# Moving background copies to another engine's DMA queue, and adding by transfer instead of by VectorE, in a one-core hybrid attention layer

## The chip, the core and the metric

The kernel runs on one core of a Trainium2 chip. The core has five engines with instruction streams of their own: TensorE (PE, matrix products; PEld are its weight loads), VectorE (DVE), ScalarE (ACT), GpSimd (POOL) and SyncE (SP). Each executes its stream in order and waits on semaphores. Sixteen DMA engines move data between the chip's memory (DRAM) and the core's SBUF; SP, ACT and POOL put transfers on queues for them. In the profile SP's transfers are on queue q1 (hardware_dynamic), POOL's on q0 (software_dynamic). An issued transfer runs by itself; whoever needs it waits until it has landed. The metric is the device time of one execution, in microseconds (us). Before the change its median is 899.32 us over three runs (899.3 to 900.65).

## The reference

One decoder layer in float32: 512 tokens, width 2048. Two groups of eight attention heads, one MLA and one FoX (with a forget gate), share one input projection `w_in` and one output projection `w_out`:

```python
h = _rms_norm(x, g_pre)
proj = h @ w_in
...
o_mla = _mla_branch(q_lat, kv_lat, k_rope_raw, g_q, w_uq, g_kv, w_ukv, cos, sin) * jax.nn.silu(gate_mla)
o_fox = _fox_branch(fq, fk, fv, f_logit, b_forget) * jax.nn.silu(gate_fox)
o = jnp.concatenate([o_mla, o_fox], axis=-1) @ w_out
return x + _rms_norm(o, g_post)
```

## The kernel before

**Three products for one.** Every float32 operand is split into a high part in PE's fast float format (`hi`, by a cast on ACT) and the rest (`lo`, by a subtraction on DVE). `mm3` (L149) then makes hi x hi, hi x lo and lo x hi, so a product step of 128 contracted rows for two output tiles is six matmuls. Weights go through this in chunks of 512 KB: `load` brings a chunk into a tile `raw`, `divide` casts it to `whi` (L277) and subtracts into `wlo` (L280). `whi` and `wlo` have three buffers each (pool `wp`), so the cast of a chunk writes where the cast three chunks earlier wrote. `chunk(i)` loads some four chunks ahead and divides two ahead of PE.

**Fewer block products.** The projections of the FoX values (v), the latents (l), the MLA gate (m) and the output (o, in two halves 0 and 1) are done as 2 x 2 block products by a scheme with seven products in place of eight. It needs sums of weight blocks:

- t7 = b12 + b22, t6 = b11 + t7, t4 = b21 + t6, t5 = b11 + b12 (up to signs, which the operand side carries).
- Most sums are made in the background in DRAM, each by a plain copy of the first block into a DRAM tile and a second transfer that adds the other block to it (`accum_op=ALU.add`). For v, l and m these are t7 and t6, 512 KB each, for four row pairs; for o they are t7, t6 and t4 over both halves, 1 MB each. They stand in the list `bg`, 36 steps.
- The sums t4 and t5 of v, l and m, and t5 of o, are made late: `load` brings the first block to `raw` and the second to a tile `second`, both on SP, and `join` adds them on DVE (L267). The products that use t5 of w_out are `("g5", 0)` and `("g5", 1)`, four chunks each.

**The pace of the background.** `paced` (L533) counts product steps; every `pace` of them (twice as many where the tile is 1 MB) it calls `add_step(n, mark)`. That call issues three things: the accumulate of step n - 1 on POOL (L310), the copy of step n on SP (L313), and a **mark** for step n + 1 on SP (L315). A mark is a transfer of 16 numbers from the `whi` tile that PE is using into the DRAM tile that the next copy will overwrite. Its data mean nothing: it makes the copy wait until the mark has landed, and the mark wait until that `whi` was cast, so that the background follows PE's progress. Since the mark reads `whi`, the cast that reuses its buffer must wait until the mark has landed. The pace is 20, 8 and 12 in the projections up to some 217 us, 4.9 in the FoX heads that follow (four product steps a chunk there), and 4.5 and 3 from some 560 us.

Within each engine and queue the order of instructions is set by a scheduler that goes by program order and readiness; `keep_in_program_order` (`in_order`, L132) fixes some of them. POOL's queue also has the transfers that put intermediate operands away in DRAM (`awaymg`, `awayoa`, `awayog`, `v_away`, `l_away`) and, at the end, adds of the residual x (L1600).

Of the kernel before, what the change touches and what calls it, by code (L numbers as in the profile page):

```python
# [16 lines left out]
ALU = mybir.AluOpType  # L17
# [49 lines left out]
def tile_hybrid_layer(  # L67
# [16 lines left out]
    nc = tc.nc  # L84
    pe, act, dve, pool = nc.tensor, nc.scalar, nc.vector, nc.gpsimd
# [14 lines left out]
    def slot(name, dt=F32, shape=(P, 2, S)):  # L100

        return sp.tile(list(shape), dt, tag="s", name=name)
# [13 lines left out]
    def split(src, name, scale=None, first=0):  # L116

        both = slot(name, F32R)
        hi, lo = both[:, 0, :], both[:, 1, :]
        split_into(hi[:, first:], lo[:, first:], src[:, first:], scale)  # L120
        return hi, lo
# [10 lines left out]
    def in_order(*instructions):  # L132

        for i in instructions:
            tc.keep_in_program_order(i)
# [72 lines left out]
    def add_chunks(w, cols, nk, per, width, first_k=0, single=0):  # L208


        first = len(chunks)
        k = 0
        while k < nk:
            n = min(1 if k < single else per, nk - k)
            chunks.append((w, cols, first_k + k, n, width))
            k += n
        return range(first, len(chunks))
# [6 lines left out]
    def raw_tile(i):  # L224
        if deep and deep[1] <= i < deep[2] and (i - deep[1]) % (DEEP + 3) < DEEP:
            return deep[0].tile([P, 1024], F32, tag="raw", name=f"raw{i}", bufs=DEEP)
        if i <= prods["g7", "v"][-1] and i % 5 < 2:
            return vr.tile([P, 1024], F32, tag="raw", name=f"raw{i}", bufs=2)
        pool = more[0] if more and (i - more[1]) % 6 < 3 else wp
        return pool.tile([P, 1024], F32, tag="raw", name=f"raw{i}", bufs=3)  # L230

    def load(i, small=None):

        w, cols, k, n, width = chunks[i]
        assert state["step"] >= needs.get(i, -3) + 2
        if cols is None:

            raw = raw_tile(i)
            to = raw if len(w.shape) == 2 else raw.rearrange("p (k c) -> p k c", k=2)
            nc.sync.dma_start(to, w)  # L240
            raws[i] = raw
            if k is not None:
                if seconds:
                    pool, bufs = seconds
                    second = pool.tile([P, 2, 512], F32, tag="second", name=f"second{i}", bufs=bufs)
                else:
                    second = slot(f"second{i}")
                nc.sync.dma_start(second, k)
                raws[i] = raw, second.rearrange("p k c -> p (k c)")
            return  # L250
        if i < 2:
            raw = slot(f"raw{i}", shape=(P, 1024))
        else:
            raw = raw_tile(i)
        v = raw[:, : n * width].rearrange("p (k c) -> p k c", k=n)
        for at, off, cnt in cols:
            (nc.sync if cnt >= P or small is None else small).dma_start(
                v[:, :, at : at + cnt],
                w[0, k * P : (k + n) * P, off : off + cnt].rearrange("(k p) c -> p k c", p=P),
            )  # L260
        raws[i] = raw
# [28 lines left out]
    def chunk(i, ahead_load=4, ahead=2):  # L290
        upto = i + ahead_load
        if deep:
            upto = max(upto, min(i + DEEP + 2, deep[2] - 1, state["loaded"] + i % 2))
        while state["loaded"] < min(len(chunks), upto + 1):
            load(state["loaded"])
            state["loaded"] += 1
        prepare(i + ahead)
        for k in range(i + ahead + 1, min(state["loaded"], i + ahead + (3 if deep else 2))):
            join(k)
        return ready.pop(i)  # L300

    W, made = {}, {}
    bg = []

    def add_step(n, mark):


        if n > 0:
            to, _, second = bg[n - 1]
            pool.dma_start(to.rearrange("p (k c) -> p k c", k=2), second, accum_op=ALU.add)  # L310
        if 0 <= n < len(bg):
            to, first, _ = bg[n]
            nc.sync.dma_start(to.rearrange("p (k c) -> p k c", k=2), first)  # L313
        if n + 1 < len(bg):
            nc.sync.dma_start(bg[n + 1][0][0:1, 0:16], mark)  # L315

    def sum_blocks(g, block, late, width=512):

# [14 lines left out]
    prods = {}  # L333
# [34 lines left out]
    first = add_chunks(w_in, [(0, O_KR - L4, KL), (KL, O_F, NH)], NK, 2, KL + NH, single=2)  # L368
# [81 lines left out]

    load_x_tile(0)
    load(0, act)
    load_x_tile(1)
    load(1, act)
    load_x_part(1)
    load(2, act)
# [76 lines left out]
    def paced(w):  # L533

        if state["step"] <= len(bg):
            state["tiles"] += 1
            wide = 0 <= state["step"] < len(bg) and bg[state["step"]][0].shape[1] > 1024
            pace = state["pace"] * (1 + wide)
            if state["tiles"] >= pace:
                state["tiles"] -= pace  # L540
                add_step(state["step"], w[0:1, 0, 0:16].bitcast(F32))
                state["step"] += 1
# [510 lines left out]
    def fox_k(p, wholes):  # L1053
        kb = [proj_bank(f"fk{p}{i}") for i in range(2)]
        proj_T(fox[p]["k"], [(kb[i], P, two[i]) for i in range(2)], hh, hl)
        k = []
        for i in range(2):
            t = tmp(f"fkt{p}{i}")
            dve.tensor_tensor(out=t, in0=kb[i], in1=rrow, op=ALU.mult)
            k.append(split(t, f"fk{p}{i}"))  # L1060
            whole_block(wholes, 2 + i, t)
        return k
# [164 lines left out]
    k = fox_k(0, wholes)  # L1227
# [27 lines left out]
    for p in range(4):  # L1255
        if p:
# [6 lines left out]
            k = fox_k(p, wholes)  # L1263
# [237 lines left out]
    for p in range(4):  # L1501
        c = mla[p]
# [46 lines left out]
        k = [[split(kb[i], f"mk{p}{i}"), tuple(keys_turned)] for i in range(2)]  # L1549
# [240 lines left out]
```

## Time and profile before

| | us |
|---|---|
| median of the timed runs | 899.32 |
| the profiled execution, whole | 901.18 |
| its span, first to last instruction | 899.4 |
| around the span | 1.8 |
| PE busy | 885.4 |
| DVE busy | 648.1 |
| ACT busy | 456.5 |
| POOL busy | 66.0 |

The page's second part cuts the span in 40 slices of 22.5 us; a digit is the busy share in tenths:

```profile
PE   9999999999999999999999999999999999999996
DVE  4579995548656636476588898965876885988786
ACT  6944434334344424335545565535565676646383
POOL 1010110011111201010000000000000000000021
DMA  9698798889899999896899884799743237789778
```

The rows of a wait view read: engine, line, what it waited for, us in total, times, longest. In a row of the timeline the first two numbers are the start and the duration, and the bracket holds the idle time before it and what ended it; an SPq row is an instruction of SP's queue. Where rows by stretches are shown, the columns are the stretch, its length, busy time and count (x) of PE, PEld, DVE, ACT and POOL, PE's granted clock, the DMA engines' mean busy share, and GB/s.

### The profile page before, as it was taken

To read this page: it belongs to the slowest core of one execution; us is meant where nothing else is said; L and a number is where in the kernel's file an instruction comes from. 1 tells how busy PE (TensorE), PEld (TensorE's weight loads), DVE (VectorE), ACT (ScalarE), POOL (GpSimd) and SP (SyncE) were. 2 spreads that over 40 slices of the span, in tenths; PEclk is the share of its full clock that TensorE was granted. 3 is DMA by queue.
4 is the path that set the end of the run, shared out by engine and by line. 5 is a ranking of instruction groups with operands and counts; after the bars stand their busy time and mean duration, and the time that the engine had idled before them with its cause. 6 is when DMAs were issued, how large, how long until landed. Compare 5 with 4: busy or idle time off the path is not lost.

```text
span 899.4 us, 12809 instructions
## 1 busy us (share of the span) xinstructions
PE 885.4 (98%) x4594; PEld 755.4 (84%) x4594; DVE 648.1 (72%) x1083; ACT 456.5 (51%) x830; POOL 66.0 (7%) x86
## 2 busy tenths in 40 slices
PE   9999999999999999999999999999999999999996
PEld 8988887888888888888998998788888888887885
DVE  4579995548656636476588898965876885988786
ACT  6944434334344424335545565535565676646383
POOL 1010110011111201010000000000000000000021
PEclk9999999999999999999999999999999999999999
DMA  9698798889899999896899884799743237789778
GB/s 299 223 268 238 207 336 283 248 225 315 256 278 274 250 246 256 249 251 174 278 411 395 318 299 134 154 232 219 208 101 125 63 118 227 228 320 319 264 214 252
DMA packets 126811, 219.31 MB, mean 244 GB/s; under 512 B 16506, under 2 KB 55188, under 8 KB 125724
## 3 DMA queue, kind: packets, MB, share of 16 engines
q1 hardware_dynamic: 114636, 180.52, 61.3%
q0 software_dynamic: 11376, 37.75, 20.0%
q8 instruction: 36, 0.59, 0.3%
q10 hardware_dynamic: 736, 0.22, 0.1%
q14 instruction: 27, 0.22, 0.1%
HBM read 203.77 MB, written 65.03 MB: 299 GB/s over the span
## 4 chain that ended last, share of the span: by engine, by line
PE 85%; DVE 5%; DMA 5%; ACT 3%; issue 1%; DVEq 0%; ACTq 0%; SPq 0%
PE fq L150 3%; PE fk L150 3%; PE fk L152 3%; PE fk L151 3%; PE fq L152 3%; PE fq L151 3%; PE in L586 3%; PE fg L150 3%; PE fg L151 3%; PE fg L152 3%; PE sm L629 2%; DMA second<-in_w_in_dram 2%; PE oa L152 2%; PE oa L151 2%; PE oa L150 2%; DVE wlo L280 2%
## 5 line engine op out<-in xcount | busy, mean ns | idle before, releaser
L280 DVE TENSOR_TENSOR wlo<-raw,whi 128x1024 fp32r<-128x1024 f32 (+3 forms) x217 | 257.1, 1188 | 139.2 <-ACT whi L277 128.1
L277 ACT CAST whi<-raw 128x1024 fp32r<-128x1024 f32 (+3 forms) x217 | 221.2, 1023 | 231.6 <-PE fk L151 35.4
L150 PE MATMUL fk<-h,whi 128*128 128x512 f32 x128 | 52.5, 410 | 0.0
L150 PE MATMUL fq<-h,whi 128*128 128x512 f32 x128 | 50.8, 397 | 0.0
L150 PE MATMUL fg<-h,whi 128*128 128x512 f32 x128 | 50.3, 393 | 0.0
L152 PE MATMUL fk<-h,wlo 128*128 128x512 f32 x128 | 50.2, 392 | 0.0
L151 PE MATMUL fk<-h,whi 128*128 128x512 f32 x128 | 50.1, 392 | 0.0
L152 PE MATMUL fq<-h,wlo 128*128 128x512 f32 x128 | 50.0, 390 | 0.0
L151 PE MATMUL fq<-h,whi 128*128 128x512 f32 x128 | 49.9, 390 | 0.0
L152 PE MATMUL fg<-h,wlo 128*128 128x512 f32 x128 | 49.9, 390 | 0.0
L151 PE MATMUL fg<-h,whi 128*128 128x512 f32 x128 | 49.8, 389 | 0.0
L647 ACT ACTIVATE pf<-pf,stf 128x128 f32<-128x128 f32 (+3 forms) x32 | 18.0, 562 | 61.1 <-DVE stf L638 61.1
L267 DVE TENSOR_TENSOR raw<-raw,second 128x1024 f32<-128x1024 f32 x32 | 39.0, 1218 | 2.6 <-DMA second<-in_w_in_dram 1.7
L586 PE MATMUL in<-whi,h 128*128 128x328 f32 x128 | 30.0, 321 | 0.0
L150 PE MATMUL mq<-ln,whi 128*128 128x512 f32 x72 | 28.7, 399 | 0.0
L152 PEld LDWEIGHTS fk<-h,wlo 128*128 128x128 f32 x128 | 24.0, 188 | 5.5
L152 PEld LDWEIGHTS fq<-h,wlo 128*128 128x128 f32 x128 | 24.0, 188 | 5.3
L151 PE MATMUL mq<-ln,whi 128*128 128x512 f32 x72 | 28.3, 393 | 0.0
L152 PEld LDWEIGHTS fg<-h,wlo 128*128 128x128 f32 x128 | 24.0, 188 | 5.1
L152 PE MATMUL mq<-ln,wlo 128*128 128x512 f32 x72 | 28.1, 390 | 0.0
L151 PEld LDWEIGHTS fg<-h,whi 128*128 128x128 f32 x128 | 24.1, 188 | 4.7
L150 PEld LDWEIGHTS fg<-h,whi 128*128 128x128 f32 x128 | 24.1, 188 | 4.7
(568 smaller groups left out, 2431.9 us busy)
## 6 DMA issues: line engine op xcount, KB each, us to landing
raw<-in_w_in_dram SPq DMA_DIRECT2D x96, 512.0 KB
raw<-in_w_out_dram SPq DMA_DIRECT2D x32, 512.0 KB
second<-in_w_in_dram SPq DMA_DIRECT2D x24, 512.0 KB
bmg<-awaymg SPq DMA_DIRECT2D x20, 256.0 KB
awaymg<-rmg POOLq DMA_DIRECT2D x8, 512.0 KB, 7.5
raw<-t6v SPq DMA_DIRECT2D x8, 512.0 KB
t7o<-in_w_out_dram SPq DMA_DIRECT2D x4, 1024.0 KB
t7o<-in_w_out_dram POOLq DMA_DIRECT2D x4, 1024.0 KB, 11.8
```

What stands on the lines that cost most here:

```text
L150: pe.matmul(o, ah, bh, start=first, stop=False, **kw)
L151: pe.matmul(o, ah, bl, start=False, stop=False, **kw)
L152: pe.matmul(o, al, bh, start=False, stop=last, **kw)
L267: tc.keep_in_program_order(dve.tensor_tensor(out=raw, in0=raw, in1=second, op=ALU.add))
L277: cast = act.copy(hi[:, :m], raw[:, :m])
L280: dve.tensor_tensor(out=lo[:, :m], in0=raw[:, :m], in1=hi[:, :m].bitcast(F32), op=ALU.subtract)
L586: pe.matmul(banks[t][:, :n], a[k][:, tss[t]], b[:, j, :], start=k == 0 and m == 0, stop=k == NK - 1 and m == 2,)
L629: pe.matmul(s[:, :nn], a[:, qs], c[:, :nn], start=(i == 0), stop=(i == len(pairs) - 1))
L647: act.activation(p, p, AF.Exp, bias=st[:, 0:1], scale=unit, accum_out=st[:, 1:2])
```

## The change

The mark and the background copies are issued by POOL, not SP. For chunks from `("g5", 0)` on, the second block of a late sum no longer goes to a tile `second`: it is a transfer on POOL that adds to `raw` in SBUF, and `join` finds nothing to do. No bytes to be read are added or taken away. All lines of the program after L242 stand two lines later, so L310, L313, L315, L277 and L280 become L312, L315, L317, L279 and L282.

```diff
             raws[i] = raw
-            if k is not None:
+            if k is not None and i >= prods["g5", 0][0]:
+                in_order(nc.gpsimd.dma_start(raw.rearrange("p (k c) -> p k c", k=2), k, accum_op=ALU.add))
+            elif k is not None:
                 if seconds:
...
         if 0 <= n < len(bg):
             to, first, _ = bg[n]
-            nc.sync.dma_start(to.rearrange("p (k c) -> p k c", k=2), first)
+            pool.dma_start(to.rearrange("p (k c) -> p k c", k=2), first)
         if n + 1 < len(bg):
-            nc.sync.dma_start(bg[n + 1][0][0:1, 0:16], mark)
+            pool.dma_start(bg[n + 1][0][0:1, 0:16], mark)
```

How that stands in the streams is seen at two places. The first is POOL in the FoX heads, from about 250 to 300 us. The names are t7m and t6m, the background sums of the MLA gate, with a number for the tile; awayoa are attention results put away. Before, POOL holds the accumulates and the away transfers alone:

```order
L310 DMA t7m_136<-in_w_in_dram 128x2x512
L310 DMA t6m_140<-t7m_136 128x1024
L310 DMA t7m_137<-in_w_in_dram 128x2x512
L310 DMA t6m_141<-t7m_137 128x1024
L310 DMA t7m_138<-in_w_in_dram 128x2x512
L925 DMA awayoa_4125<-gf_883 256x1x256
```

Now the marks (L317, from whi) and the copies (L315) stand between them:

```order
L312 DMA t7m_136<-in_w_in_dram 128x2x512
L317 DMA t6m_140<-whi_2454 16x1x1
L315 DMA t6m_140<-in_w_in_dram 128x2x512
L312 DMA t6m_140<-t7m_136 128x1024
L317 DMA t7m_137<-whi_2515 16x1x1
L315 DMA t7m_137<-in_w_in_dram 128x2x512
L312 DMA t7m_137<-in_w_in_dram 128x2x512
L317 DMA t6m_141<-whi_2564 16x1x1
L315 DMA t6m_141<-in_w_in_dram 128x2x512
L317 DMA t7m_138<-whi_2618 16x1x1
L312 DMA t6m_141<-t7m_137 128x1024
L315 DMA t7m_138<-in_w_in_dram 128x2x512
```

Mark, copy and accumulate of one sum now follow each other on one queue; at t6m_141 the next mark stands ahead of the accumulate.

From SP all marks and background copies are gone; the loads of `raw`, key rows, values and fetched operands are left there.

The second place is SP and POOL at the products with t5 of w_out. `raw` rows are first blocks, `second` rows second blocks, bog fetched operands, t7o sums read back. SP before:

```order
L240 DMA raw_7831<-in_w_out_dram 128x2x512
L248 DMA second_7784<-in_w_out_dram 128x2x512
L959 DMA bog_7804<-awayog_4345 128x512
L248 DMA second_7808<-in_w_out_dram 128x2x512
L959 DMA bog_7829<-awayog_4185 128x512
L248 DMA second_7833<-in_w_out_dram 128x2x512
L240 DMA raw_7853<-in_w_out_dram 128x2x512
L248 DMA second_7855<-in_w_out_dram 128x2x512
L240 DMA raw_7877<-t7o_152 128x2x512
```

SP now:

```order
L240 DMA raw_7828<-in_w_out_dram 128x2x512
L961 DMA bog_7803<-awayog_4345 128x512
L961 DMA bog_7826<-awayog_4185 128x512
L240 DMA raw_7848<-in_w_out_dram 128x2x512
L240 DMA raw_7870<-t7o_152 128x2x512
```

The second blocks are the last transfers on POOL ahead of the residual adds (L1602):

```order
L312 DMA t4o_163<-t6o_159 128x2048
L243 DMA raw_7782<-in_w_out_dram 128x2x512
L243 DMA raw_7805<-in_w_out_dram 128x2x512
L243 DMA raw_7828<-in_w_out_dram 128x2x512
L243 DMA raw_7848<-in_w_out_dram 128x2x512
```

Eight `second` loads have moved from SP to POOL, and eight additions are gone from DVE.

## The prediction

> **What bounds the kernel now.** I read the page's first lines, then busy time by stretches, then what TensorE (PE) waited for, then the queues SP and POOL on which the change works.
>
> ```profile
> PE 885.4 (98%) x4594; PEld 755.4 (84%) x4594; DVE 648.1 (72%) x1083; ACT 456.5 (51%) x830; POOL 66.0 (7%) x86
> 740.00:800.00 60.00, 60.00 (x277) 49.62 (x276) 46.83 (x59) 35.16 (x52) 0.00 (x0) 1.00 0.72 234
> 217.00:312.00 95.00, 94.68 (x445) 78.75 (x445) 60.11 (x134) 39.59 (x82) 16.67 (x18) 1.00 0.97 268
> 312.00:420.00 108.00, 108.00 (x526) 90.05 (x525) 63.32 (x144) 42.05 (x92) 8.84 (x10) 1.00 0.92 247
> 790.00:845.00 55.00, 54.27 (x238) 43.84 (x237) 46.01 (x52) 26.24 (x34) 0.00 (x0) 1.00 0.89 311
> ```
>
> PE is busy in 885.4 of 899.4 us at the full clock (1.00). 277 matmuls in 60 us are 0.217 us each, without idle time. So a copy or a sum that becomes cheaper elsewhere is worth only the PE waits that it ends:
>
> ```profile
> PE mix L1625 <- ACT scaler L1624: 2.2, 1, 2.2
> PE sm L629 <- DVE stm L638: 0.9, 1, 0.9
> PE vg L151 <- DVE wlo L280: 0.8, 1, 0.8
> PE od L151 <- DVE wlo L280: 0.7, 2, 0.4
> PE vg L150 <- ACT whi L277: 0.5, 1, 0.5
> PE vp L151 <- DVE wlo L280: 0.3, 1, 0.3
> ```
>
> Mix is the kernel's end. The others come to 3.2 us, which is all that can be won. Much can be lost, though: from 217 to 420 us the 16 DMA engines are 92 to 97% busy, and that is where the moved copies run.
>
> **Part 1, copies and marks on POOL: the new wait.** Before, a copy of step n+1 (SP) and the accumulate of step n (POOL) ran side by side. After, one queue in program order holds mark, copy, accumulate. A copy waits for its mark to land, an accumulate for its copy, and in the order shown above most marks stand behind the previous accumulate, whose 16 DMA engines they share. A step becomes a series: copy, then accumulate with the next mark. What each takes:
>
> ```profile
> 303.39 0.56 SPq L313 DMA_DIRECT2D t7m<-in_w_in_dram  x1
> 308.13 1.17 POOL L310 DMA_DIRECT2D t7m<-in_w_in_dram  x1 [2.67 <-DMA t7m<-in_w_in_dram]
> 293.31 0.56 SPq L313 DMA_DIRECT2D t6m<-in_w_in_dram  x1
> 304.55 0.91 POOL L310 DMA_DIRECT2D t6m<-t7m  x1 [8.38 <-DMA t6m<-in_w_in_dram]
> ...
> t6m<-t7m POOLq DMA_DIRECT2D x4, 512.0 KB, 7.1
> t7m<-in_w_in_dram POOLq DMA_DIRECT2D x4, 512.0 KB, 9.8
> awaymg<-rmg POOLq DMA_DIRECT2D x8, 512.0 KB, 7.5
> DMA to landing us min/median/max: 5.4/9.5/14.4
> ```
>
> The last row is for all of L310. A copy's landing lets the accumulate start: at most 4.7 us after issue (303.39 to 308.13), at most 11.2 in the other pair, which shared the engines with an accumulate. No trace row has a plain 512 KB copy on POOL from DRAM to DRAM; its nearest is awaymg, 7.5. I take 4.5, by the undisturbed pair, since no other background transfer runs beside it then. An accumulate takes 5.4 at the least, 7.1 (t6m) or 9.8 (t7m, issued 1.5 to 2.7 us behind another one). I take 6.5 for one that is alone. With 0.5 for two resumptions (an estimate) a serial step takes 4.5 + 6.5 + 0.5 = **11.5 us**, bounded by 9.9 (4.5 + 5.4) and 17.3 (7.5 + 9.8). Where the order puts the next mark and copy ahead of the accumulate's successor, a step costs about the accumulate, 7 us.
>
> The program asks for a step every 4.9 products' steps, four of which use up one cast weight chunk (whi):
>
> ```profile
> L277 ACT CAST whi<-raw x9: 1037/1048/1056, 255.2 to 311.0; 128x1024 fp32r<-128x1024 f32 x9
> L277 ACT CAST whi<-raw x6: 1037/1055/1056, 222.9 to 243.1; 128x1024 fp32r<-128x1024 f32 x6
> PE fk L151: 5.7, 4
> ```
>
> Nine casts from 255.2 to 311.0 are 6.97 us a chunk, so 6.97 x 4.9 / 4 = 8.5 us a step. That is shorter than 11.5: **POOL falls behind**. Between t7l_122's mark (cast at 222.9) and t7m_136's (243.1) four steps, mostly of the short kind, cost 4 x 7 = 28 us against 20.2: about 7 late. From there to t7o_152's mark are eight steps, six serial and two short: (6 x 11.5 + 2 x 7) / 8 = 10.4, so 8 x 1.9 = 15 more. That mark then lands 5 us after its issue, behind an accumulate. Sum: 27 us after its cast.
>
> Who waits for it: the mark reads whi, which has three buffers, so ACT's third cast after it cannot start before the mark has landed. That cast is due 3 x 6.97 - 1.05 = 19.9 us later. ACT is 27 - 20 = 7 us late, and behind the cast on ACT stand the exponentials (L647) and splits (L139) that PE's transposes and value products need. Today such a cast waits for PE alone (last row), and PE had none of these waits. I let PE see 6 of the 7 us.
>
> Two other things stand behind a waiting POOL. Its away transfers (awaymg, v_away, awayoa) come later by the same lag; before 217 us a step comes only every 20, 8 or 12 product steps of six matmuls (26, 10.4 and 15.6 us at 0.217 each), so there is hardly a lag for them to take over. And the sums themselves are read late:
>
> ```profile
> L240 SPq DMA_DIRECT2D raw<-t6m x8: 319/320/418, 456.9 to 531.1; - x8
> ```
>
> t6m's last accumulate, at 319 us today, may come 100 us later before its reader waits. Only the marks bite.
>
> The 1 MB steps that follow come at half the rate, every 17 us:
>
> ```profile
> t7o<-in_w_out_dram POOLq DMA_DIRECT2D x4, 1024.0 KB, 11.8
> t6o<-t7o POOLq DMA_DIRECT2D x4, 1024.0 KB, 10.5
> t4o<-t6o POOLq DMA_DIRECT2D x4, 1024.0 KB, 8.7
> ```
>
> Mean accumulate 10.3, a copy some 7 (4.5 plus half again, an estimate), 0.5 to resume: 17.8. The lag isn't worked off; 0.8 x 5 = 4 us more. The six later o steps, from 560 us, start with an idle POOL; I count them at nothing (bound: 0.8 us each, 5 us). **Loss: 6 + 4 = 10 us.** Ends: at 9.9 a step the lag stays under 20 and the loss is 0; at 13 (copy 5.8, accumulate 6.7) the eight steps add 24 in place of 15, the 1 MB ones some 10: 25 us; at 17.3 it would be over 50.
>
> The 72 added issues are nothing in themselves: POOL is 7% busy, and an issue takes 0.9 to 1.2 us (the POOL rows above).
>
> What SP wins: marks no longer block its loads, and copies don't precede them.
>
> ```profile
> SPq L313 <- DMA t7m<-whi: 21.2, 4, 10.0
> 119.96 11.23 DMA second<-in_w_in_dram
> 608.11 12.91 DMA raw<-in_w_ukv_dram
> ```
>
> The two loads, from the chain that ended last, landed late, and waits vg (1.3 us) and sm (0.9) follow them. At 607.5 a 1 MB copy went out on SP just ahead of the second. But the engines that carry these bytes stay the same, so I count half: -1.1 us. At worst nothing.
>
> The Trainium skill, "DMA: Bandwidth & Descriptors", section "Anatomy of one DMA — SWDGE (gpsimd) path", puts a POOL-issued DMA at about 2.0 us plus bytes / 436 GB/s. By this estimate 512 KB is 3.2 us, a serial step 6.4, and the loss 0, which is the first rival below. The trace has no accumulate under 5.4 us, so the measurement speaks against it.
>
> **Part 2, the last sums by adding transfers.** Eight DVE adds go, and eight loads `second` move from SP to POOL, where nothing else is queued (idle from 653 to 868 us).
>
> ```profile
> L267 DVE TENSOR_TENSOR raw<-raw,second x8: 1216/1218/1226, 796.8 to 841.0; 128x1024 f32<-128x1024 f32 x8
> 793.38 1.41 SPq L240 DMA_DIRECT2D raw<-in_w_out_dram  x1
> 807.62 1.22 DVE L267 TENSOR_TENSOR raw<-raw,second 128x1024 f32<-128x1024 f32 x1
> 809.00 1.05 ACT L277 CAST whi<-raw 128x1024 fp32r<-128x1024 f32 x1 [2.04 <-DVE raw L267]
> c<-in_x_dram POOLq DMA_DIRECT2D x8, 256.0 KB, 10.1
> ```
>
> The adds are 8 x 1.22 = 9.8 us of DVE, hidden today but for the od wait (0.7): DVE is busy 46 of 55 us. The price is that load and sum no longer run in parallel. The fourth chunk: load out at 794.8, landed after 4.7 (the copy's row), added 7 later (between 5.4 and 10.1, the accumulates above, nearer to t6m's 7.1): ready at 806.5, against 808.8 today. With 10.1 it is 809.6, 0.8 late. So I take **-0.7 us**, bounds -1.0 and +1.6 for both blocks. The other four chunks have some 10 us of room (loads from 816.5, adds from 829.8).
>
> **Sum.** 10 - 1.1 - 0.7 = +8 us on the span of 899.4, so 907.4; with the 1.8 us around the span (901.18 for the profiled execution) 909.2. The timed median, 899.32, is 1.9 under that execution, so I predict 899.3 + 8 = **907.3**.
>
> **Rivals.**
> - *POOL keeps up (faster).* If serial steps take under about 10 us, the mark lands inside the 19.9 us and PE waits for nothing new; the waits vg, sm, od and vp shrink: 899.3 - 2.5 = 896.8. For it: copies of 4.7, an accumulate of 5.4, and DMA engines relieved by the series itself. Against: 97% DMA. Chance 0.21.
> - *The two cancel.* Lag just over 20 us, loss 1 to 3, won 1 to 2, or the background was never on PE's path either way: 899. Chance 0.15.
> - *POOL is far behind.* Steps of 13 us or more, as the loaded rows (11.2 for a copy, 9.8 for an accumulate) have it: 899.3 + 25 - 1.8 = 923 and up. Chance 0.14, of which 0.08 above 926.
> - *DVE holds up POOL's issues.* If each issue had to wait for the DVE sum that runs then (1.22 us, the L267 row), two issues a step would add 2.4 us: the six serial steps 14 us more, 899.3 + 8 + 14 = 921 or so. Against it:
>
> ```profile
> L310 POOL DMA_DIRECT2D t7m<-in_w_in_dram x4: 1172/1172/1482, 263.8 to 308.1; - x4
> ```
>
> Four issues spread by 0.3 us while DVE was busy 63% of the time. Chance 0.03, taken out of the forecast's 0.50. The Trainium skill, "SBUF — State Buffer", section "SBUF: two separate sides", states such a rule: a DVE operation in a two-port mode locks GpSimd out of writing descriptors. By that rule alone the background would be the slower the more of it POOL issues; the row shows no trace of it.
>
> **How the numbers follow.** The forecast of a loss up to 25 us has 0.50 (0.03 of it by DVE), the far case 0.14: slower 0.64, same 0.15, faster 0.21. 0.2% (1.8 us) is about what a measurement of this kernel can tell from none. Range 896 to 926: it takes in the first rival's low end and steps up to 13 us, and leaves out the worst of the far case.
>
> **What would show it.** In the profile after: accumulates on POOL waiting for copies nearly back to back from 245 us; casts of whi waiting for DMA t7m<-whi, t6m<-whi or t7o<-whi between 290 and 410 us, and PE waits behind ACT there; if none, the lag argument falls. Accumulates into raw should land within 7 us, and od should have no wait. A copy on POOL that lands in 3.5 us, or an accumulate in 5, makes the prediction wrong on the fast side.

## The result, and the profile after

The changed kernel's median is **962.97 us** (960.86 to 963.98, four runs) against 899.99 us for the kernel before on the same chip (899.3 to 905.14, four runs): a ratio of 1.0684, 95% interval 1.064 to 1.0727. It is slower by some 63 us. The forecast was 907.3 with a range up to 926. The sign is right, and so is the mechanism of part 1; the size is far off, and part 2 lost time where a gain was forecast.

First what answers to the opening lines of the prediction: the page's busy time, and busy time by stretches in the FoX heads, which are later now.

```profile
PE 902.7 (94%) x4594; PEld 763.5 (80%) x4594; DVE 638.3 (67%) x1075; ACT 456.5 (48%) x830; POOL 119.8 (12%) x166
```

```profile
245.00:310.00 65.00, 54.94 (x248) 44.17 (x247) 28.07 (x67) 20.76 (x48) 12.97 (x18) 0.95 0.79 206
310.00:365.00 55.00, 43.09 (x192) 34.48 (x191) 19.81 (x43) 14.08 (x32) 11.82 (x17) 0.91 0.77 177
365.00:430.00 65.00, 54.11 (x240) 43.58 (x239) 29.06 (x68) 20.36 (x45) 8.77 (x12) 0.92 0.82 197
```

PE lacks 10, 12 and 11 us in these three stretches; before, it was full there. DVE and ACT are idler too (POOL isn't), and so are the DMA engines: 77 to 82% and 177 to 206 GB/s, where before they showed 92 to 97% and 247 to 268. So nothing is overloaded here; something waits. PE's largest waits:

```profile
PE pvf L150 <- ACT phf L139: 21.0, 5, 9.1
PE sf L631 <- ACT fw L127: 7.1, 1, 7.1
PE od L151 <- DVE wlo L282: 6.0, 8, 0.8
```

PE waits for splits (L139) and copies (L127) of ACT and for what comes of chunks that are ready late. ACT's own waits at the cast of `whi`:

```profile
ACT whi L279 <- issue: 61.9, 17, 10.9
ACT whi L279 <- DMA raw<-in_w_out_dram: 26.8, 8, 6.0
...
ACT whi L279 <- DMA t7m<-whi: 18.2, 2, 9.9
```

18.2 us are for marks by name, and 61.9 us are put down to "issue", a wait whose releaser the row doesn't name. The times at which the marks land name it: by the trace, 14 casts that stood between 249 and 411 us before start 0.06 to 0.16 us after a mark lands, and the five longest "issue" waits are theirs. The row of raw is part 2: all eight chunks with an adding transfer are waited for.

To see where the time arises I compare the two executions cast by cast: 217 casts of weights stand in the same order in both, and the delay is the start of a cast after less its start before. These are my differences, in us:

```
cast starts before at   211.2  270.2  311.0  364.8  420.7  459.1  613.2  634.8  785.6  814.0  838.8  882.4
delay after the change    2.1    5.9   26.5   45.0   50.7   52.6   53.1   50.8   50.5   55.0   58.6   59.6
```

Of the 52.6 us at 459, some 50 arise between 211 and 427 us, in the FoX heads; 2.3 come back from 621 on; 9.1 are added in the two t5 products of w_out at the end. The last delay is the difference of the spans, 959.1 - 899.4 = 59.7.

**How one lag turns into one delay.** Two marks show it, each with the cast before and after that is the third next behind it. First casts of the kernel before, on ACT: of the chunk whose whi t7o_152's mark reads (310.95) and its third next (330.26), then the same pair for the mark of t4o_161 (391.25, 410.73).

```profile
310.95 1.04 ACT L277 CAST whi<-raw 128x1024 fp32r<-128x1024 f32 x1
330.26 1.05 ACT L277 CAST whi<-raw 128x1024 fp32r<-128x1024 f32 x1 [0.84 <-PE fk L151]
391.25 1.05 ACT L277 CAST whi<-raw 128x1024 fp32r<-128x1024 f32 x1 [0.89 <-PE fk L151]
410.73 1.06 ACT L277 CAST whi<-raw 128x1024 fp32r<-128x1024 f32 x1
```

After the change, POOL's timeline with these two marks and the copies that follow them, and below it the two third next casts in ACT's timeline:

```profile
363.93 0.81 POOL L317 DMA_DIRECT2D t7o<-whi  x1
370.60 0.72 POOL L315 DMA_DIRECT2D t7o<-in_w_out_dram  x1 [5.86 <-issue]
...
453.07 0.97 POOL L317 DMA_DIRECT2D t4o<-whi  x1
...
463.09 0.71 POOL L315 DMA_DIRECT2D t4o<-in_w_out_dram  x1 [8.30 <-DMA t4o<-whi]
```

```profile
369.34 1.04 ACT L279 CAST whi<-raw 128x1024 fp32r<-128x1024 f32 x1 [9.38 <-issue]
...
462.87 1.05 ACT L279 CAST whi<-raw 128x1024 fp32r<-128x1024 f32 x1 [6.40 <-PE fg L152]
```

By the trace the marks land at 369.27 and 462.80; the casts start 0.07 us later. (The last row names PE, whose release came at 462.71; the wait in ACT's queue ahead of it ran from 455.92 until the mark landed.) The first mark lands 58.3 us after the time of its cast before, the deadline is 330.26 - 310.95 = 19.3, and the delay is 39.1. The second: 71.6 late, deadline 19.5, delay 52.1. The lag less the deadline is the loss. Where a cast starts as the mark lands, that sum comes out by itself; what the two casts show is that they do start there.

**Why the lag is so much larger than forecast.** POOL's timeline after, in two pieces: one as forecast, one not.

```profile
292.09 0.82 POOL L317 DMA_DIRECT2D t7m<-whi  x1
298.20 0.72 POOL L315 DMA_DIRECT2D t7m<-in_w_in_dram  x1 [5.29 <-issue]
302.69 1.17 POOL L312 DMA_DIRECT2D t7m<-in_w_in_dram  x1 [3.77 <-DMA t7m<-in_w_in_dram]
303.41 0.96 POOL L317 DMA_DIRECT2D t6m<-whi  x1
...
323.01 1.15 POOL L312 DMA_DIRECT2D t7m<-in_w_in_dram  x1 [7.37 <-DMA t7m<-in_w_in_dram]
323.73 1.88 POOL L927 DMA_DIRECT2D awayoa<-gf  x2
324.93 1.20 POOL L317 DMA_DIRECT2D t6m<-whi  x1
337.70 0.72 POOL L315 DMA_DIRECT2D t6m<-in_w_in_dram  x1 [11.57 <-DMA t6m<-whi]
...
342.65 0.84 POOL L317 DMA_DIRECT2D t7m<-whi  x1
```

From mark to mark, 292.09 to 303.41, is a serial step of 11.3 us: the accumulate with the mark behind it some 6.1, the copy 4.5. That is the step that the prediction worked out. But from 324.93 to 342.65 it takes 17.7: two away transfers stand between accumulate and mark, and the mark's 64 bytes landed 12.5 us after their issue. By the trace the four landed in the order of their issue, at 335.95, 336.60, 337.25 and 337.41; in the whole trace none of POOL's 151 transfers landed before one issued earlier. From t7m_136's mark (261.18) to t7o_152's (363.93) eight steps take 102.75 us, 12.8 each.

### The profile page after: what moved, and what is told of

Read it like the earlier page. It is cut to its first block, busy times and chain, and to the rows that moved or that the text cites. A ratio compares the mean times of both kernels' runs of the same rounds, so it can differ in the third digit from the quotient of the medians.

```text
span 959.1 us, 12763 instructions
## 1 busy us (share of the span) xinstructions
PE 902.7 (94%) x4594; PEld 763.5 (80%) x4594; DVE 638.3 (67%) x1075; ACT 456.5 (48%) x830; POOL 119.8 (12%) x166
## 4 chain that ended last, share of the span: by engine, by line
PE 45%; DMA 5%; issue 3%; DVE 2%; ACT 1%; POOL 0%; DVEq 0%; POOLq 0%; ACTq 0%
DMA raw<-in_w_out_dram 4%; PE sm L631 3%; PE oa L152 2%; PE oa L151 2%; PE oa L150 2%; PE mq L150 1%; PE mq L151 1%; PE mq L152 1%; DMA t4o<-whi 1%; PE od L151 1%; PE od L152 1%; PE ptm L658 1%; PE gl L150 1%; PE od L150 1%; PE mv L150 1%
## 5 line engine op out<-in xcount | busy, mean ns | idle before, releaser
L282 DVE TENSOR_TENSOR wlo<-raw,whi 128x1024 fp32r<-128x1024 f32 (+3 forms) x217 | 257.2, 1188 | 220.8 <-ACT whi L279 212.5
L279 ACT CAST whi<-raw 128x1024 fp32r<-128x1024 f32 (+3 forms) x217 | 221.1, 1023 | 311.0 <-issue 61.9
L150 PE MATMUL fq<-h,whi 128*128 128x512 f32 x128 | 52.3, 409 | 0.0
L151 PE MATMUL fq<-h,whi 128*128 128x512 f32 x128 | 51.0, 398 | 0.0
L269 DVE TENSOR_TENSOR raw<-raw,second 128x1024 f32<-128x1024 f32 x24 | 29.3, 1219 | 2.4 <-DMA second<-in_w_in_dram 2.4
L243 POOL DMA_DIRECT2D raw<-in_w_out_dram x8 | 9.5, 1188 | 164.8 <-DVE rog L885 123.8
L151 PEld LDWEIGHTS fq<-h,whi 128*128 128x128 f32 x128 | 24.9, 195 | 4.7
L150 PEld LDWEIGHTS fq<-h,whi 128*128 128x128 f32 x128 | 24.9, 194 | 4.7
L150 PEld LDWEIGHTS fk<-h,whi 128*128 128x128 f32 x128 | 24.7, 193 | 4.5
```

What stands on the lines that cost most here:

```text
L150: pe.matmul(o, ah, bh, start=first, stop=False, **kw)
L151: pe.matmul(o, ah, bl, start=False, stop=False, **kw)
L243: in_order(nc.gpsimd.dma_start(raw.rearrange("p (k c) -> p k c", k=2), k, accum_op=ALU.add))
L269: tc.keep_in_program_order(dve.tensor_tensor(out=raw, in0=raw, in1=second, op=ALU.add))
L279: cast = act.copy(hi[:, :m], raw[:, :m])
L282: dve.tensor_tensor(out=lo[:, :m], in0=raw[:, :m], in1=hi[:, :m].bitcast(F32), op=ALU.subtract)
```

## Experiments

Each stands against the kernel before (median 899.7 to 900.8, run beside it each time). p1 names copies and marks on POOL alone, with the last sums as before; p2 the last sums alone. In the kernels named p1 the lines keep their old numbers up to L315.

**The parts alone.** p1_only keeps the hunk in `add_step`, p2_only the one in `load`.

> Copies and marks on POOL, the last sums of w_out on VectorE as before. Theory A (POOL's series of mark, copy and accumulate lets the marks fall behind, and each late mark keeps a whi buffer from ScalarE's next cast): the delay of the changed kernel up to its 420th us of the old time, 52.6 us, less some 2 us won where a w_ukv load lands earlier: 899.5 + 50.5 = 950 us. Rival B (the adding transfers at the end cost most, or both parts only together): under 930 us.

> Only the last sums by adding transfers on POOL; copies and marks on SP as before. If the parts add up, casts of the eight chunks come 9 us later in all, as in the changed kernel: 908 us. If the 9 us there came from the background having been late, this is 899 to 900 us, or 898.5 as the prediction had it.

p1_only: 950.61 us (948.94 to 953.77), ratio 1.0548 (1.0516 to 1.058). p2_only: 909.13 (907.51 to 909.48), 1.008 (1.0057 to 1.0103). Both are as expected if the parts add up. Against 900.77 that is +49.8 and +8.4, together 58 of the 63 us. Part 1 delays the casts by 51.7 us at 459 and 49.5 after 635, part 2 adds nothing up to 785 us and 7.9 from there to the end. Both together showed 52.6 and 9.1 at these places.

**Copies or marks.** Each kernel moves one of the two to POOL:

```diff
copies_pool
-            nc.sync.dma_start(to.rearrange("p (k c) -> p k c", k=2), first)
+            pool.dma_start(to.rearrange("p (k c) -> p k c", k=2), first)
marks_pool
-            nc.sync.dma_start(bg[n + 1][0][0:1, 0:16], mark)
+            pool.dma_start(bg[n + 1][0][0:1, 0:16], mark)
```

> Of part 1 only the copies are on POOL; the marks are back on SP, so a late POOL no longer holds a mark and its whi buffer. Theory A: POOL still falls behind by tens of us, but TensorE does not wait for it: 897 to 901 us, no cast waits for a mark for longer than 2 us. Rival C (the copies on POOL's queue are slower, or crowd the DMA engines, and the weights come late): 930 to 950 us, as with both.

> Of part 1 only the marks are on POOL, behind the accumulates; the copies are back on SP. Theory A: marks again land behind accumulates and hold whi, but the copies run beside the accumulates, so a step takes some 8 to 9 us instead of 12: 5 to 30 us lost, 905 to 930 us. Rival C (it is the copies on POOL): 899 to 901 us.

copies_pool: 901.87 (897.68 to 904.19), ratio 1.0004 (0.9983 to 1.0024); its profiled execution is not late in the FoX heads (-1.5 us at 421), is 5.7 us later at 613 than at 459, and ends 2.3 late. marks_pool: 940.48 (937.64 to 942.11), 1.0428 (1.0399 to 1.0458), more than expected. So 36 copies of 0.5 or 1 MB on POOL's queue are in the median no loss and no gain that can be told; 36 transfers of 64 bytes there lose 40 us. With both there (p1_only) a mark also stands behind the copies, and the loss is 50.

**A fourth buffer for whi.** If the hold is what costs, one buffer more gives one chunk more.

```diff
-NSLOT = 28
+NSLOT = 27
-        hi = wp.tile([P, 1024], F32R, tag="whi", name=f"whi{i}")
+        hi = wp.tile([P, 1024], F32R, tag="whi", name=f"whi{i}", bufs=4)
```

> Copies and marks on POOL, last sums on VectorE, as in p1_only (950.6 us), with a fourth buffer for whi (and 27 slots in place of 28 elsewhere, to make room). Theory A (a mark holds its whi buffer until it lands, and the cast that wants the buffer is the third next): the deadline of every mark moves by one chunk, once, 6.97 us where it decides: 943.6 us, and the delay of the casts against before about 45.5 after 421 us in place of 52.4. Rival B (PE loses the time to the late background itself, by transfers that crowd or results that are missing, not by the hold): no change, 949 to 953.

943.66 us (941.76 to 945.75), the expected figure. The way there was less even: the delay is 5.4 us at 311 (p1_only 23.9), 36.9 at 421, 45.4 at 459 and 40.5 at the end, 10 under p1_only. The missing slot also shifts the work ahead of the FoX heads (-2.6 us at 211), and the last cast gains 10 us on p1_only's, the whole span only 7.3. So this run supports the hold, but that its time meets the expected figure to the digit is in part luck.

**A slower pace in the FoX heads.**

```diff
-    set_pace(4.9)
+    set_pace(7)
```

> As p1_only, but in the FoX heads a background step is asked for every 12.2 us (1.75 chunks) in place of 8.5. Theory A (the loss is the excess of the chain's time per step over the pace, less the deadline of 19.9 us): eight steps at 12.8 against 12.2 lose 5 us of lag, and the start lag of 15 us stays under the deadline with it; the chunks behind these lose little: 899 to 915 us, with casts delayed by under 15 us at 421 us. The price is that some steps move to later stages, where the pace isn't changed. Rival B (copies and marks on POOL cost PE time by themselves, whatever the pace): 940 to 950.

913.76 us (911.22 to 918.12), ratio 1.0156 (1.0126 to 1.0187): asked for less often, the same chain loses 17.8 us at 421 in place of 51.0. The time is inside the 899 to 915 expected, though the delay is over its 15 us: the eight steps from t7m_136's mark (273.41) to t7o_152's (383.71) take 13.8 us each here, not 12.8, and so miss the 12.2 asked by 13 us in all in place of the 5 reckoned.

**Marks that hold nothing, first try: a constant.**

```diff
-            pool.dma_start(bg[n + 1][0][0:1, 0:16], mark)
+            pool.dma_start(bg[n + 1][0][0:1, 0:16], ident[0:1, 0:16])
```

> As p1_only, but the mark reads a constant (the identity's first row) in place of the cast whi, so that it holds no buffer of the casts; the values that it writes are overwritten by the copy as before. What is left out is the pacing by TensorE's chunks: the chain runs as fast as POOL and the buffers of the sums let it. Theory A (the hold is the whole mechanism): the casts no longer wait for any mark, 895 to 910 us, the top end if the earlier start of the transfers crowds the loads. Rival B (the chain's own traffic or its lateness costs the time): 940 us and more.

1030.51 us (1027.34 to 1032.44): theory A's figure is missed, and the rival's "940 and more" takes it in, but by a cause that neither named. Without the pacing most of the series runs in the first third. ACT's waits up to 400 us:

```profile
ACT whi L277 <- DMA raw<-in_w_in_dram: 53.4, 10, 11.0
ACT smg L139 <- DMA awaymg<-rmg: 40.8, 1, 40.8
ACT L700 <- DMA awaymg<-rmg: 19.8, 1, 19.8
```

From 0 to 110 us the DMA engines are full (a share of 1.01, 0.85 before) and PE works 88 us, loads of weights come late, and two waits of 40.8 and 19.8 us are for away transfers that stand on POOL behind the series. All 133 us have arisen by the cast that starts at 364 us (231 before), none later. The run shows what the marks are for, but it leaves the question open, since no series was left where p1_only loses its time.

**Second try: the mark reads a copy.** The pacing stays, whi is free as soon as ACT has copied 16 numbers.

```diff
+            copied = cst.tile([1, 16], F32, tag="copied", name=f"copied{n}", bufs=8)
+            act.copy(copied, mark)
-            pool.dma_start(bg[n + 1][0][0:1, 0:16], mark)
+            pool.dma_start(bg[n + 1][0][0:1, 0:16], copied)
```

> As p1_only (950.6 us), but each mark reads a copy of 16 numbers that ScalarE takes of whi at the same place, in one of eight buffers of its own: the pacing by the chunks stays, the mark holds no whi. ScalarE gets 35 copies of some 0.1 to 0.2 us. Theory A (the hold of whi is the mechanism): the series on POOL still falls behind by about 10 us for each 3 steps, but no cast waits for a mark; 896 to 906 us, with the delay of the casts under 5 us at 421 us. Rival B (the late series itself costs TensorE, by crowding or by results that come late): 925 us and more, with waits for raw in place of those for marks.

939.3 us (934.16 to 944.7), ratio 1.0433 (1.0393 to 1.0473): by its time the rival is right and theory A wrong. The trace says something else. First the stretches, as shown for the changed kernel above:

```profile
245.00:310.00 65.00, 65.00 (x311) 54.18 (x310) 37.59 (x91) 26.84 (x65) 13.48 (x18) 1.00 0.86 218
310.00:365.00 55.00, 55.00 (x264) 45.64 (x263) 30.56 (x72) 21.96 (x52) 11.29 (x15) 1.00 0.78 199
365.00:430.00 65.00, 64.89 (x353) 55.59 (x352) 41.24 (x87) 28.74 (x62) 8.00 (x11) 1.00 0.82 205
430.00:480.00 50.00, 34.48 (x239) 31.95 (x237) 20.84 (x23) 14.05 (x19) 5.92 (x8) 0.89 0.91 276
```

In the three stretches where the changed kernel loses 33 us PE is full, at the full clock; the delay is -0.1 at 421 us. Yet the series is just as late: t7o_152's mark is issued at 363.4, in the changed kernel at 363.93. ACT's copies for the marks take 0.2 us each. So the hold on whi was the whole loss there: the late series alone, with its traffic and its away transfers, costs PE nothing up to 430 us. Then comes, unexpected, one wait on ACT's timeline, and POOL's timeline says why:

```profile
499.20 0.58 ACT L1435 COPY lat<-gl 128x512 f32<-128x512 f32 x1 [39.59 <-DMA awayog<-rog]
```

```profile
482.61 0.88 POOL L310 DMA_DIRECT2D t4o<-t6o  x1 [9.62 <-DMA t4o<-in_w_out_dram]
483.16 0.89 POOL L927 DMA_DIRECT2D awayog<-rog  x1
...
484.32 1.52 POOL L927 DMA_DIRECT2D awayog<-rog  x2
```

The first two transfers of rog, which before went out at 435.8 and 439.3, stand in order behind the late series and go out at 483.2 and 484.3. By the trace the second lands at 499.12, and ACT's `lat`, which wants a slot that is being put away, starts 0.08 us later: ACT has stood 39.6 us.

**Both places closed, in two ways.** p1_copied_pace7 adds the pace of 7 to the copied marks; p1_copied_away_act instead lets ACT issue the away transfers of w_out's group:

```diff
-            pool.dma_start(to.rearrange("p (h c) -> p h c", c=HALF), src)
+            (act if of == "o" else pool).dma_start(to.rearrange("p (h c) -> p h c", c=HALF), src)
```

> Marks read copies as in p1_mark_copied (939.3 us), and in the FoX heads a step is asked for every 12.2 us as in p1_pace7 (913.8 us). Theory A (the lag of the series is paid where something waits in order behind it: at the casts by the marks' hold on whi, or at ScalarE's latent by the transfer of rog that POOL issues behind the series): the hold is gone, and with 12.2 us asked the series should be done by about 445 us, so that the transfer of rog is late by less than the 14 us of room that it has in before (landed 446, ScalarE needs the slot at 459): 897 to 904 us. Rival B (further places where the late series is paid): 908 and more.

> As p1_mark_copied (939.3 us, of it 39.6 in one wait of ScalarE for the transfer of rog queued behind the series), with the transfers away of w_out's group issued by ScalarE's queue in place of POOL's. The series stays as late as it was. Theory A: no one waits behind the series any more, the wait of 39.6 goes: 897 to 906 us, the top end if ScalarE's own issues (0.5 to 1.2 us each, and waits for VectorE's rog) delay casts. Rival B (the late series is paid at another place once this one is gone, by the slots that the later steps hold, say): 915 and more.

p1_copied_pace7: 904.23 us (901.13 to 909.57), ratio 1.0052 (1.0033 to 1.0071), at the upper end of theory A's 897 to 904 and just over it. Its profiled execution shows a delay of 0.1 us at 421, 2.8 at 459 and 0.4 at 882: there copies and marks on POOL cost nearly nothing, since the series keeps its pace. Of the 4 us that the timed runs are over before, that execution shows one (a span of 900.3); where the rest lies isn't known. p1_copied_away_act: 918.03 (916.47 to 918.41), 1.0192 (1.0175 to 1.0209); the rival was right. The wait for rog is gone, and 19 us are lost all the same, from 441 to 504 us. ACT's largest wait from 435 to 510 us, the stretch there, and the same stretch in the kernel before:

```profile
ACT whi L277 <- DMA raw<-in_w_in_dram: 16.7, 5, 5.3
```

```profile
440.00:505.00 65.00, 51.32 (x291) 43.69 (x290) 34.01 (x35) 23.20 (x28) 5.33 (x7) 0.95 1.04 353
```

```profile
440.00:490.00 50.00, 50.00 (x313) 45.34 (x312) 36.65 (x36) 25.41 (x30) 1.06 (x2) 1.00 1.04 411
```

This stage had its DMA engines full before, at 411 GB/s, without any background. The end of the late series, up to 498 us, now runs through it, and the weights come late. That reading is argued from these rows, and p1_copied_pace7 speaks for it, whose series is done by 444.5 us and which loses 2.8 us there; a run with the same away transfers and no late series was not made.

**Half of part 2.** Only the odd chunks are finished by an adding transfer; copies and marks are on SP.

```diff
-            if k is not None:
+            if k is not None and i >= prods["g5", 0][0] and i % 2:
+                in_order(nc.gpsimd.dma_start(raw.rearrange("p (k c) -> p k c", k=2), k, accum_op=ALU.add))
+            elif k is not None:
```

> Copies and marks on SP as before; of each block of w_out in the last group only the odd chunks are finished by an adding transfer into SBUF, the even ones by VectorE. p2_only was 909.13 us. Theory A2 (latency: the first such transfer is ready 10 to 11 us after its issue, and each then costs 4.0 us against 3.6 us per chunk of TensorE, so that four in a row fall behind): one transfer for two chunks has 7.2 us for its 4.0 us of throughput, and only the latency counts, which the even chunk ahead of it covers in part: 900 to 904 us. Rival B2 (each adding transfer costs TensorE about 1.1 us wherever it stands, 9 us for eight): 904.5 us, with the delay growing at each odd chunk.

903.41 us (901.7 to 905.34), ratio 1.0038 (1.0023 to 1.0052). From issue to landing its four adding transfers take 8.2 to 9.7 us (median 8.4), the eight of p2_only 8.6 to 11.4 (9.2). The delay goes from -2.5 us to 2.6 in the first block of four, and it ends at 2.2; in p2_only it goes from -2.0 to 3.9 and then to 5.9. So the loss in the second block is gone where an even chunk lies between two transfers, and that in the first block is little smaller (5.1 us against 5.9). There it arises at the third chunk first (-2.9 to 0.5): by the trace its load took 7.6 us and its addition 9.7. The time of 903.41 hardly tells A2 (900 to 904) from B2 (904.5); but a growth at each odd chunk, as B2 had it, isn't there.

No kernel of the study is faster than the one before.

## Why the prediction was wrong

**What bounds the kernel; what can be won.** Right that PE bounds it; the 3.2 us that could be won were put to no test, since no run won any. SP's gain was put at 1.1 us; the delay falls by 2.3 at 621 us, where the load of w_ukv came late before. p1_only shows the same fall, but p2_only, with its marks on SP, has one of 1.3 there too, so how much of it is SP's isn't settled.

**Part 1, the mechanism.** Right: chain, lag, hold on whi, third next cast. copies_pool, marks_pool and p1_mark_copied each confirm a piece. That PE would see 6 of ACT's 7 us was too mild; it sees all of it.

**Part 1, the sum.** This is the step that failed: "27 us after its cast" was 58.3. Three terms were mis-sized.

| term | predicted | measured |
|---|---|---|
| lag when t7m_136's mark is issued | 7 | 18 (261.18 - 243.1), four steps of 8.75 in place of 7, and 3 at their start |
| eight steps, over the 8.5 asked | 8 x 1.9 = 15 | 102.75 - 67.9 = 35 |
| from issue to landing of t7o_152's mark | 5 | 5.3 |
| lag; less the deadline | 27 - 20 = 7 | 58.3 - 19.3 = 39 |
| 1 MB steps | 4 | 52.1 - 39.1 = 13 |

The serial step was about right: 11.5 predicted, 11.3 (292.09 to 303.41) and 12.4 (279.65 to 292.09) measured. Wrong was what the other steps take. The two pairs counted at 11.5 + 7 = 18.5 us took 21.5 and 21.3: a mark ahead of an accumulate saves 1.6 us (two serial steps would be 23), not 4.5. And two of the other four steps took 18.5 and 17.7, with marks that landed 10.4 and 12.5 us after their issue, one behind an accumulate of t7l, one behind away transfers. The prediction saw those transfers only as sufferers ("come later by the same lag"); they are also part of the queue. For the 1 MB steps the 17.8 us were exact (17.83 from 363.93 to 453.07, five steps); but they were asked for every 16.06 us ((391.25 - 310.95) / 5), not 17, which is 8.8 us over five, and the last mark took 9.7 us to land in place of 5.3.

A loss that is a small difference, 27 less 20, doubles with 10% more on each of eight steps of 10.4 us. The range allowed 13 us for a serial step, but left the start at 7 and the short steps at 7; with the measured start and steps the same sum is 18 + 35 + 5 - 19 = 39. No row had shown a short step, and its bounds should have stood beside the others.

**Away transfers.** "Only the marks bite" is true of the changed kernel, and only because the marks bite first: they hold PE back, so the series is never later against PE than the deadline of some 19 us. Freed of them (p1_mark_copied) the same lag is paid at `awayog`, 39.6 us, and freed of that (p1_copied_away_act), as far as the rows above show, in the loads of the next stage.

**Part 2.** The sign was wrong: 9.1 us in place of -0.7. Two terms failed, "landed after 4.7" and "added 7 later", and od, which should have had no wait, has 6.0 us in eight. By the trace the fourth chunk's load goes out at 842.34 and lands at 854.12, 11.8 us later (POOL's last row below stands 7.14 us for it), and its addition takes 8.9 more; in p2_only the two take 11.3 and 9.2. Even before the change that load took 8.3 us (793.38 to 801.70), which cost nothing there, since the second block was on its way beside it. The 4.7 came from a copy in the FoX heads. The timeline after, POOL's adding transfers of the first block and the casts of their chunks on ACT:

```profile
840.29 1.24 POOL L243 DMA_DIRECT2D raw<-in_w_out_dram  x1 [123.77 <-DVE rog L885]
842.77 1.17 POOL L243 DMA_DIRECT2D raw<-in_w_out_dram  x1 [1.25 <-ACT whi L279]
846.41 1.19 POOL L243 DMA_DIRECT2D raw<-in_w_out_dram  x1 [2.46 <-DMA bog<-awayog]
854.74 1.17 POOL L243 DMA_DIRECT2D raw<-in_w_out_dram  x1 [7.14 <-DMA raw<-in_w_out_dram]
```

```profile
851.72 1.05 ACT L279 CAST whi<-raw 128x1024 fp32r<-128x1024 f32 x1 [5.97 <-DMA raw<-in_w_out_dram]
855.69 1.05 ACT L279 CAST whi<-raw 128x1024 fp32r<-128x1024 f32 x1 [2.92 <-DMA raw<-in_w_out_dram]
859.73 1.05 ACT L279 CAST whi<-raw 128x1024 fp32r<-128x1024 f32 x1 [2.99 <-DMA raw<-in_w_out_dram]
863.78 1.05 ACT L279 CAST whi<-raw 128x1024 fp32r<-128x1024 f32 x1 [2.48 <-DMA raw<-in_w_out_dram]
```

The first lands 11.3 us after its issue (851.62), and its cast is 3.1 us late (851.72 against 798.16 before plus the delay of 50.5); the next ones are 4.0 us apart, where before they stood 3.6 apart. In p2_only the first is in time, and the others fall behind:

```profile
795.75 1.05 ACT L279 CAST whi<-raw 128x1024 fp32r<-128x1024 f32 x1 [2.47 <-DMA raw<-in_w_out_dram]
800.59 1.05 ACT L279 CAST whi<-raw 128x1024 fp32r<-128x1024 f32 x1 [3.79 <-DMA raw<-in_w_out_dram]
805.76 1.04 ACT L279 CAST whi<-raw 128x1024 fp32r<-128x1024 f32 x1 [4.12 <-DMA raw<-in_w_out_dram]
811.10 1.04 ACT L279 CAST whi<-raw 128x1024 fp32r<-128x1024 f32 x1 [3.77 <-DMA raw<-in_w_out_dram]
```

These casts stand 4.8, 5.2 and 5.3 us apart. Their third and fourth transfer go out at 796.54 and 801.81, within 0.7 us of the landing of the loads that they add to (795.88 and 801.19): load and addition stand in series, and both are slow. The DMA engines are full meanwhile, a share of 1.03 at 281 GB/s from 787 to 812 us, where the kernel before showed 0.88 at 307 GB/s from 790 to 815. So what the prediction had wrong is the price of the series under this load, and it worked out the fourth chunk by itself, not the spacing. How much is due to the adding and how much to POOL's queue wasn't tried. Nor did the second block have "10 us of room": before, its first load landed at 823.54, 6.3 us ahead of the add at 829.8, and after the change the first transfer there took 10.4 us; the delay rises by another 4.6 (55.0 to 59.6).

**Rivals.** "POOL keeps up" and "the two cancel" are out by the ratio of 1.0684. "POOL is far behind" is what happened, at 963 and not 923; but the plain serial steps took 11.3 and 12.4, not 13 and more, and the longer ones had other transfers of the queue in them. DVE holding up issues plays no part that shows: L312's four issues of t7m take 1150 to 1182 ns, the four of L310 before 1172 to 1482. The estimate from the Trainium skill, "DMA: Bandwidth & Descriptors" (section "Anatomy of one DMA — SWDGE (gpsimd) path"), 3.2 us for 512 KB, isn't met by any such transfer on POOL's queue in the changed kernel: by the trace a copy takes 4.0 us at the least (287.03 to 291.00), an accumulate 5.3.

## What to carry to other kernels

A transfer that reads a tile holds it until it has landed. On a queue that is worked in order it goes out behind all that stands before it, and on POOL's it landed behind all that too: put a small transfer that paces or releases something on a queue where nothing long precedes it, or let it read a copy of its own. Before work is chained on one queue, compare the time of a whole step, with every other transfer of that queue in it, to the interval at which it is asked for; the excess adds up step by step, and once the slack is used up each microsecond of it is lost at the first place that waits in order. Ask then what the second place is, since closing the first only moves the payment.

## What the runs showed of the hardware

- A transfer of 64 bytes on POOL's queue took between 1.6 and 12.5 us to land, 7.1 in the median; the same marks on SP's queue before took 1.0 to 11.7, 3.7 in the median. The two longest on POOL, 12.5 and 11.9 us, each stood behind an accumulate and two away transfers. None of POOL's 151 transfers landed before one that was issued earlier.
- An adding transfer of 512 KB from DRAM into SBUF takes 8.4 to 12.2 us from issue to landing in the medians of three kernels, and queued one behind another they end 4.0 us apart in the changed kernel; by the trace, the plain loads of the same second blocks on SP took 6.1 to 8.1 before.
- PE's granted clock, 1.00 in all stretches shown before, is 0.91 to 0.95 in the stretches of the FoX heads in which PE waits, and 1.00 again in the same stretches of p1_mark_copied. Which of the two brings about the other wasn't tried; the waits account for the delay without it.
